# Held weights of eleven groups of stages at offsets of 8 to 112 bytes in place of one offset of 64 bytes, in a two-model transformer kernel on one core

## The chip, the cores and the metric

The kernel runs on one core of a Trainium2 chip. The time is the device time of one execution in microseconds (us); three runs give a median. One further execution was profiled, and every row below comes from it.

## The reference, cut to what matters

Fourteen sublayers run one after another on a sequence of 256 tokens of width 1024, in float32: a mixer, a cross-attention and a gated feed-forward net, twice, and then twice a feed-forward net, a three-branch mixer, a cross-attention and a second feed-forward net. Each ends in a residual sum and a layer norm. Nearly all of the arithmetic is products of the activations with weight matrices, such as

```
def swiglu_ffn(x, w_in, w_out):
    a, b = jnp.split(x @ w_in, 2, axis=-1)
    return (jax.nn.silu(a) * b) @ w_out
```

with a hidden width of 2816. Attention, scans and norms are small beside them.

## The kernel before, in words

A product is made of three matmuls in the type fp32r. Each operand is split into a high part (the value cast to fp32r) and a low part (the value less the high part), and the sum is high times high, low times high and high times low. All weights are 725 blocks of 128 partitions by 1024 words. `Stream._load` brings one into one of four staging tiles `w` by a DMA on SP's queue (lines 200 to 206). `Stream._split` casts it on ScalarE (L230) and subtracts on VectorE (L231) into one of ten slots of the pool `wp`, tile `w2`; the high part starts at `off`, the low part 1024 words, that is 4096 bytes, behind it. A slot is 2048 + 2*16 words, 8320 bytes, which is 65 times 128 bytes, so that all slots lie alike towards 128 bytes.

There are two ways to use a block. In `unit_group` (L360, L362, L364) the weights are held: a block of eight 128x128 pieces is loaded into the array piece by piece (a weight load, LDWEIGHTS) and the 256 columns of the activations `xT` stream past each (a MATMUL). One block makes 24 matmuls of 256 columns, called a unit here. `mm3` (L319 to L321) is also used with held weights, by the keys of a cross-attention (`x*_k`, `y*_k`), by the gates `e_g` and by the branches of the mixer (`m*_br`, which also come to 24 matmuls of 256 columns a block). In the other way, `mm3` holds activations (`xT`, `ph`, `pl`, or the memory's block) and streams the weights past: the down projections `_d`, the output projections `_o`, the values `_v` and the first 256 columns of a feed-forward net, `_t`.

The set `STANDING` names the endings of the held blocks; `stands(name)` tells whether a block is one. A block that is streamed, and the memory's block, lies at offset 0 of its slot; a held block lies at `HALF`, 16 words, that is 64 bytes. The pieces of a held block are 512 bytes apart and the pieces of `xT` 1024 bytes apart, so that towards 128 bytes each piece lies like the first.

The name of a block is the stage, an underscore and the part: `h10_g` is the gate and up projection of the feed-forward net `h10`. The stages run in the order e, x0, f0, o, x1, f1, h00, m0, y0, h01, h10, m1, y1, h11. Held blocks by stage: e has 17; x0 and x1 have 16 each (8 of `_q`, 8 of `_k`); f0, f1, h00, h01, h10 and h11 have 40 each (`_g`); o has 16 (`_qk`); m0 and m1 have 66 each (`qa` 4, `ckv` 1, `iq` 4, `ik` 1, `s` 8, `c` 12, `gate` 24, `br` 12); y0 and y1 have 8 each. That is 453 blocks. In a feed-forward net the order is gate unit, up unit, then 15 streamed matmuls of a down block of two units before, with the activation function in between on ScalarE and VectorE.

The order of the instructions on each engine is written out by the program; the blocks' order (`plan`) is recorded in a first pass and the loads and splits run ahead of their use by as many slots as are free (`pump`).

Of the kernel before, what the change touches and what calls it, by code (L numbers as in the profile page):

```python
# [168 lines left out]


HALF = 16


def stands(name):

    return name.split("_", 1)[-1] in STANDING
# [24 lines left out]
class Stream:  # L201
# [20 lines left out]
    def _split(self):  # L222
        n = self.net
        cols = self.plan[self.split][2]
        w = self.stage.pop(self.split)
        off = HALF if stands(self.plan[self.split][0]) else 0
        both = n.wp.tile([128, 2048 + 2 * HALF], F32R, tag="w2", name="w2")
        hi, lo = both[:, off:off + 1024], both[:, off + 1024:off + 2048]
        self._low()
        n.nc.scalar.copy(hi[:, :cols], w[:, :cols])  # L230
        self.due = lambda: n.nc.vector.tensor_sub(lo[:, :cols], w[:, :cols], hi[:, :cols].bitcast(F32))  # L231
        self.parts[self.split] = (hi, lo)
        self.split += 1
        self.live += 1
# [1364 lines left out]
```

## Time and profile before

| | us |
|---|---|
| median of 3 runs | 2263.19 |
| lowest and highest | 2262.1, 2263.37 |
| the profiled execution's own time | 2261.28 |
| its span, from first to last instruction | 2259.6 |
| TensorE busy in it | 2227.5 |
| VectorE busy | 1495.2 |
| ScalarE busy | 1155.4 |

The profiled execution lies 1.9 us under the median, and 1.7 us of its time lie outside the span. PE is TensorE's matmuls, PEld its weight loads, which overlap them; DVE is VectorE, ACT is ScalarE, POOL is GpSimd, SP the engine whose queue carries the loads. The matmuls are pipelined: one of 256 columns is shown with some 280 ns although the next one starts some 115 ns after it. So the pace is read from the starts of matmuls that follow one another, and not from their durations.

### The profile page before, as it was taken

What the parts mean: (1) busy time and instruction counts of PE and PEld (TensorE: products, weight loads), DVE (VectorE), ACT (ScalarE), POOL (GpSimd) and SP (SyncE); (2) the same over time, 40 slices, a digit from 0 to 9 for tenths busy, and PEclk for the clock granted to TensorE, in tenths of its full rate; (3) what the DMA queues carried; (4) which work ended last, traced back from release to release, by engine and by line L of the source; (5) the groups of instructions that cost most, each with busy time, mean ns of one, the idle gap of its engine ahead of it and who ended that gap; (6) DMA issues with size and microseconds to landing.
All of it is one profiled execution on the core that took longest, in us unless ns stands there. A gap on an engine that the chain in (4) does not pass through costs nothing.

```text
span 2259.6 us, 40982 instructions
## 1 busy us (share of the span) xinstructions
PE 2227.5 (99%) x16600; PEld 2083.7 (92%) x16600; DVE 1495.2 (66%) x2270; ACT 1155.4 (51%) x1856; POOL 203.7 (9%) x239
## 2 busy tenths in 40 slices
PE   8999999999999999999999999999999999999998
PEld 6989999988999999999899999999999899999998
DVE  5886665677657567656486677656656477677655
ACT  5555454378545444444745554444543845545542
POOL 0720000011000000000202100000000101200000
PEclk9999999999999999999999999999999999999999
DMA  8655476464446654764355655764764446555762
GB/s 235 169 168 168 151 255 191 154 207 138 159 151 233 191 186 166 229 190 152 131 179 158 198 176 192 231 189 136 253 192 144 159 144 183 169 194 167 258 191 77
DMA packets 118080, 407.50 MB, mean 180 GB/s; under 512 B 14169, under 2 KB 19418, under 8 KB 117890
## 3 DMA queue, kind: packets, MB, share of 16 engines
q1 hardware_dynamic: 116258, 402.00, 54.8%
q0 software_dynamic: 768, 1.57, 0.7%
q8 instruction: 130, 2.13, 0.4%
q10 hardware_dynamic: 864, 1.31, 0.2%
q14 instruction: 60, 0.49, 0.1%
HBM read 403.76 MB, written 1.06 MB: 179 GB/s over the span
## 4 chain that ended last, share of the span: by engine, by line
PE 91%; DVE 3%; ACT 3%; DMA 2%; issue 1%; POOL 1%; ACTq 0%; DVEq 0%; SPq 0%; POOLq 0%
PE ps L360 15%; PE ps L362 15%; PE ps L364 15%; PE acc L319 7%; PE acc L320 7%; PE acc L321 7%; PE ps L319 5%; PE ps L321 5%; PE ps L320 5%; DVE w L231 1%; PE ps L563 1%; PE ps L739 1%; PE ps L759 1%; ACT w L230 1%; DMA w<-in_o_qk 1%
## 5 line engine op out<-in xcount | busy, mean ns | idle before, releaser
L231 DVE TENSOR_TENSOR w<-w,w 128x1024 fp32r<-128x1024 f32 x725 | 883.3, 1238 | 363.5 <-ACT w L230 361.0
L360 PE MATMUL ps<-xT,w 128*128 128x256 f32 x3232 | 904.7, 280 | 0.0
L364 PE MATMUL ps<-xT,w 128*128 128x256 f32 x3232 | 897.1, 278 | 0.0
L362 PE MATMUL ps<-xT,w 128*128 128x256 f32 x3232 | 897.1, 278 | 0.0
L230 ACT CAST w<-w 128x1024 fp32r<-128x1024 f32 x725 | 748.4, 1051 | 223.7 <-PE ps L364 123.9
L360 PEld LDWEIGHTS ps<-xT,w 128*128 128x128 f32 x3232 | 608.2, 188 | 10.0 <-issue 5.5
L364 PEld LDWEIGHTS ps<-xT,w 128*128 128x128 f32 x3232 | 607.2, 188 | 0.0
L362 PEld LDWEIGHTS ps<-xT,w 128*128 128x128 f32 x3232 | 606.6, 188 | 0.6
L319 PE MATMUL acc<-w,ph 128*128 128x512 f32 (+1 forms) x940 | 329.5, 351 | 0.6 <-ACT ph L307 0.6
L320 PE MATMUL acc<-w,ph 128*128 128x512 f32 (+1 forms) x940 | 327.9, 349 | 0.0
L321 PE MATMUL acc<-w,pl 128*128 128x512 f32 (+1 forms) x940 | 327.6, 348 | 0.0
L319 PEld LDWEIGHTS acc<-w,ph 128*128 128x128 f32 x940 | 177.2, 189 | 25.7 <-ACT ph L307 0.8
L320 PEld LDWEIGHTS acc<-w,ph 128*128 128x128 f32 x940 | 177.0, 188 | 24.4
L321 PEld LDWEIGHTS acc<-w,pl 128*128 128x128 f32 x940 | 176.8, 188 | 24.2 <-DVE pl L308 0.2
L534 POOL TENSOR_TENSOR col<-col,mhalf 128x1 f32<-128x1 f32 (+1 forms) x38 | 28.5, 751 | 1559.2 <-DVE col L542 1437.1
L575 ACT ACTIVATE k<-ps 128x256 f32<-128x256 f32 x120 | 45.9, 383 | 160.4 <-PE ps L364 160.4
L304 ACT CAST ph<-k 128x256 fp32r<-128x256 f32 x120 | 48.8, 407 | 132.5 <-DVE k L577 132.5
L319 PE MATMUL ps<-w,w 128*128 128x256 f32 x384 | 111.8, 291 | 0.0
L319 PE MATMUL ps<-w,xT 128*128 128x256 f32 (+1 forms) x304 | 102.0, 336 | 9.2 <-ACT w L230 9.2
L321 PE MATMUL ps<-w,w 128*128 128x256 f32 x384 | 107.8, 281 | 0.0
L320 PE MATMUL ps<-w,w 128*128 128x256 f32 x384 | 107.5, 280 | 0.0
L576 DVE SCALAR_TENSOR_TENSOR k<-k,ps 128x256 f32<-128x256 f32 x120 | 50.4, 420 | 78.2 <-ACT k L575 78.2
(265 smaller groups left out, 2487.1 us busy)
## 6 DMA issues: line engine op xcount, KB each, us to landing
w<-in_h_g SPq DMA_DIRECT2D x160, 512.0 KB, 4.3
w<-in_h_d SPq DMA_DIRECT2D x88, 512.0 KB, 4.3
w<-in_f_g SPq DMA_DIRECT2D x80, 512.0 KB, 4.3
w<-in_m_gate SPq DMA_DIRECT2D x48, 512.0 KB, 3.9
w<-in_f_d SPq DMA_DIRECT2D x44, 512.0 KB, 4.2
gb<-in_ln_row SPq DMA_DIRECT2D x28, 512.0 KB, 6.8
w<-in_m_c SPq DMA_DIRECT2D x24, 512.0 KB, 3.2
w<-in_m_br SPq DMA_DIRECT2D x24, 512.0 KB, 3.6
```

The lines of the kernel that those rows point to most:

```text
L230: n.nc.scalar.copy(hi[:, :cols], w[:, :cols])
L231: self.due = lambda: n.nc.vector.tensor_sub(lo[:, :cols], w[:, :cols], hi[:, :cols].bitcast(F32))
L304: nc.scalar.copy(hi, src)
L319: mm(ps, a[0], b[0], start=first, stop=False)
L320: mm(ps, a[0], b[1], start=False, stop=False)
L321: mm(ps, a[1], b[0], start=False, stop=last)
L360: mm(ps, ws[i][0][:, k, :], xh[:, k, :], start=k == 0, stop=False)
L362: mm(ps, ws[i][1][:, k, :], xh[:, k, :], start=False, stop=False)
L364: mm(ps, ws[i][0][:, k, :], xl[:, k, :], start=False, stop=k == 7)
L534: self.nc.gpsimd.tensor_tensor(y, v, self.mhalf[:, :n], op=OP.pow)
L575: nc.scalar.activation(h, pg, AF.Tanh, scale=0.5)
L576: nc.vector.scalar_tensor_tensor(h, in0=h, scalar=1.0, in1=pg, op0=OP.add, op1=OP.mult)
```

## The change

The offset of a held block is taken from a table by the stage's name, in words of 4 bytes, with `HALF` for the stages that are not in it (e, y0, y1). For h01 and m1 the table has the 16 words of before. In bytes: f0 16, f1 32, h00 48, h01 64, h10 80, h11 96, m0 112, m1 64, x0 32, x1 96, o 8. Streamed blocks stay at 0. Nothing else changes, neither the instructions nor their order.

```
+BESIDE = dict(f0=4, f1=8, h00=12, h01=16, h10=20, h11=24, m0=28, m1=16, x0=8, x1=24, o=2)
...
-        off = HALF if stands(self.plan[self.split][0]) else 0
+        name = self.plan[self.split][0]
+        off = BESIDE.get(name.split("_")[0], HALF) if stands(name) else 0
         both = n.wp.tile([128, 2048 + 2 * HALF], F32R, tag="w2", name="w2")
         hi, lo = both[:, off:off + 1024], both[:, off + 1024:off + 2048]
```

## Rows read from the trace of the kernel before

**Rows 1.** The page: busy time of each engine, and the granted clock by slices.
```profile
PE 2227.5 (99%) x16600; PEld 2083.7 (92%) x16600; DVE 1495.2 (66%) x2270; ACT 1155.4 (51%) x1856; POOL 203.7 (9%) x239
...
PEclk9999999999999999999999999999999999999999
```

**Rows 2.** The page: the chain that ended last, shares by engine.
```profile
PE 91%; DVE 3%; ACT 3%; DMA 2%; issue 1%; POOL 1%; ACTq 0%; DVEq 0%; SPq 0%; POOLq 0%
```

**Rows 3.** Groups by line and form: busy us, mean ns, idle us before and releasers.
```profile
L360 PE MATMUL ps<-xT,w 128*128 128x256 f32 x3232 | 904.7, 280 | 0.0
...
L360 PEld LDWEIGHTS ps<-xT,w 128*128 128x128 f32 x3232 | 608.2, 188 | 10.0 <-issue 5.5 <-ACT sp L1180 0.7 <-ACT ph L304 0.7
```

**Rows 4.** Timeline of PE: start us, us, instruction. Two units: from first to next first.
```profile
741.67 0.28 PE L360 MATMUL ps<-xT,w 128*128 128x256 f32 x1
741.78 0.28 PE L362 MATMUL ps<-xT,w 128*128 128x256 f32 x1
741.90 0.28 PE L364 MATMUL ps<-xT,w 128*128 128x256 f32 x1
...
744.39 0.28 PE L360 MATMUL ps<-xT,w 128*128 128x256 f32 x1
...
758.16 0.28 PE L360 MATMUL ps<-xT,w 128*128 128x256 f32 x1
...
760.98 0.28 PE L360 MATMUL ps<-xT,w 128*128 128x256 f32 x1
```

**Rows 5.** Timeline of PE: the first and the last of the 404 units.
```profile
54.95 0.28 PE L360 MATMUL ps<-xT,w 128*128 128x256 f32 x1
...
57.77 0.28 PE L360 MATMUL ps<-xT,w 128*128 128x256 f32 x1
...
2232.64 0.28 PE L360 MATMUL ps<-xT,w 128*128 128x256 f32 x1
...
2235.36 0.40 PE L319 MATMUL acc<-w,ph 128*128 128x512 f32 x1
```

**Rows 6.** Timeline of PE: values of x1, memory's block held, weights streamed, both at 0.
```profile
620.48 0.28 PE L319 MATMUL ps<-w,w 128*128 128x256 f32 x1
...
623.33 0.49 PE L658 MATMUL ps<-sq,s 128*128 128x128 f32 x3
```

**Rows 7.** The chain in order of time, 208 to 220 us: start, us, what.
```profile
209.18 0.44 PE ps L658 x4
209.62 1.73 PE ps L739 x8
```

**Rows 8.** Windows: f0, f1, h00, h01, h10 whole; us, busy by engine (instructions), clock, DMA.
```profile
264.16:449.37 185.21, 185.21 (x1404) 176.60 (x1403) 120.13 (x156) 87.10 (x116) 4.05 (x4) 1.00 0.61 195
678.54:863.76 185.22, 185.22 (x1404) 176.54 (x1403) 120.03 (x156) 87.06 (x116) 4.07 (x4) 1.00 0.60 194
864.24:1049.41 185.17, 185.17 (x1404) 176.44 (x1403) 120.00 (x156) 86.99 (x116) 4.12 (x4) 1.00 0.61 197
1372.89:1558.71 185.82, 185.82 (x1404) 177.30 (x1402) 118.96 (x153) 86.90 (x116) 3.59 (x4) 1.00 0.60 193
1559.19:1744.87 185.68, 185.68 (x1404) 176.94 (x1403) 120.04 (x156) 86.69 (x116) 4.11 (x4) 1.00 0.61 196
```

**Rows 9.** Lines L230 and L231: duration ns min/median/max, first and last start.
```profile
L230 ACT CAST w<-w x725: 1027/1050/1092, 6.0 to 2226.3; 128x1024 fp32r<-128x1024 f32 x182
...
L231 DVE TENSOR_TENSOR w<-w,w x725: 1153/1225/2043, 7.1 to 2227.4; 128x1024 fp32r<-128x1024 f32 x182
```

**Rows 10.** Waits of PE: for whom, us in total, times, longest.
```profile
PE ps L319 <- ACT w L230: 9.2, 2, 7.1
PE ps L563 <- POOL x L550: 6.9, 10, 2.0
```

## The prediction

> **What bounds the kernel now.** I read the page's busy times first: PE is busy for 2227.5 of 2259.6 us, all of it at the high one of the two clocks, 2.4 GHz, in each of the 40 slices [rows 1]. The chain that ended last is PE for 91% of the span [rows 2], and the waits of PE for other engines are a few us in all [rows 10]. So the time is the number of matmuls by their pace, and whatever changes the pace of a long series of matmuls comes out in the total nearly whole.
>
> The mean durations do not tell the pace: 280 ns for a matmul of 256 columns [rows 3], while the next starts 110 to 120 ns on. The timeline does. In a unit of f1 24 matmuls take 744.39 - 741.67 = 2.72 us, 113.3 ns each; in another unit of the same stage they take 760.98 - 758.16 = 2.82 us, 117.5 ns each [rows 4]. Nothing waits in either, and both hold weights at the same 64 bytes. Inside a unit the step is steady from first to last, so there are two levels at which the stream can settle. The first of the 404 units is of the slow kind, 2.82 us, and the last of the fast kind, 2.72 us [rows 5]; over all 404, waits left out, the mean step is 115.1 ns, with about 61 in 100 steps at 113 or 114 ns and 38 in 100 at 117 ns or more.
>
> What differs where distance is zero? In the values of x1 the held block and the streamed one both lie at the start of a slot. There 24 matmuls of the same size take 623.33 - 620.48 = 2.85 us, 118.8 ns each [rows 6], more than either level of the held weights. A weight load (128 words a partition) runs while the matmul before it reads its 256 columns, and the two readers go through the same memory side by side. I take it that the difference between 118.8 and 115.1 ns, 3.7 ns a matmul, is what the 64 bytes now save, though the rows also differ in which tensor is held.
>
> **The change, part by part.** No instruction is added, removed or moved: same loads, splits and matmuls, same queues and waits. What changes is the start of held blocks in their slots. Held blocks with a new distance: 5 feed-forward nets of 40, m0 with 66, x0, x1 and o with 16 each, 314 in all, by 24 = 7536 matmuls. The other 139 (e 17, h01 40, m1 66, y0 and y1 8 each) keep 64 bytes and are the control.
>
> The trace has only two distances between a held fp32r block and what streams past it, 0 and 64 bytes. None of the new ones is shown, so the price of each is bounded from both sides. The upper end is the step at 0, 118.8 ns: 7536 x 3.7 = 28 us slower. The lower end is the fastest pace at which any 128-column load and matmul go here: four transposes take 0.44 us, 110 ns each, and eight attention matmuls of plain float32 and 256 columns take 1.73 us, 216 ns each or 108 ns a half [rows 7]; at 108 ns the 7536 would be 54 us faster. That end is far from every fp32r row. The nearer one is that all settle at the 113.3 ns of the fast unit: 1.8 x 7536 = 13.6 us faster.
>
> Between ends I take the row that each distance is nearest to, by a straight line: 64 bytes is the farthest that two places can be apart on a ring of 128, so a block 16 bytes from either end of the ring keeps a quarter of the saving, one at 32 a half, one at 48 three quarters. A unit has 24 x 3.7 = 89 ns to lose. Then f0 (16 bytes, three quarters of 40 x 0.089) loses 2.7 us; f1 (32) 1.8; h00 (48) 0.9; h10 (80) 0.9; h11 (96) 1.8; m0 (112, three quarters of 66) 4.4; x0 and x1 (32, 96) 0.7 each; o (8 bytes, seven eighths of 16) 1.2. The sum is 15.1 us. By the chain's share, 91% of it ends on the path: 13.7 us. In the feed-forward nets nothing can hide it, for PE is busy without a gap [rows 8]; in m0, o and the attention a part falls beside the waits of PE for a softmax or a load, which is what the other 9% stand for.
>
> The Trainium skill speaks against any effect at all: SBUF — State Buffer, section "Who interferes with whom", gives TensorE two independent read ports, one for the moving operand and one for the weight load, and says that it never waits on anyone. By that rule the sum would be nil; the two levels at one distance and the higher one at zero [rows 4, 6] do not look like it, but no row here changes the distance alone.
>
> The other edits cost nothing. The cast takes 1027 to 1092 ns for all 725 blocks, those at 0 and those at 64 bytes alike, and the subtraction has one median, 1225 ns, with a tail to 2043 [rows 9]; if a start at 8 bytes lengthened both by half, as no row says, it would be 0.5 and 0.6 us a block for o's 16 blocks, under a unit's 2.7 us. In a feed-forward net DVE is busy for 120 of 185 us and ACT for 87 [rows 8], so the splits have room; without it a unit would wait for its block, 1.2 us each. Loads, slots and the order on SP's queue are as before, and DMA writes the staging tiles, which don't move.
>
> **The sum.** The profiled execution took 2261.3 us, 1.9 under the median of 2263.2. 2261.3 + 13.7 = 2275.0, and against the median 2276.9. I say 2277.
>
> **The rivals.** First, no change (2259 to 2268): what counts is only that the two do not start alike, and every distance from 8 to 112 bytes does what 64 does. For it: the slow and the fast level both occur at 64, so which one a unit falls into hangs on more than the distance; the same stage at the same distance takes 185.17 us in h00 and 185.82 in h01 [rows 8], a drift of 0.65 us that needs no cause in the offsets. It is also what comes out where the two readers don't meet at all, so that rows 6 is slow for another reason, and where the slots' own place or the streamed tiles' place makes the distance another than the label says. Against it: the 3.7 ns would then jump within 8 bytes.
>
> Second, on the other side, faster: 64 bytes was one of the places, not the best, and other distances hold the stream at the fast level throughout. The place is the 24 matmuls of a unit; the price is 115.1 - 113.3 = 1.8 ns for each of 7536, 13.6 us, 12.4 on the path, and so 2250.8 against the median. It decides from a mean of 0.6 ns less on the 7536, 4.5 us, that is when a good third of the slow units turns fast with none turning slower. For it: 38 in 100 steps are slow now, so there is something to gain at some place, and the farthest place on the ring need not be the one where the load keeps clear of a stream that reads 256 words while it reads 128. Against it: all the new distances would have to be as good as the best of the old, while seven of the nine groups go nearer to zero by 32 bytes or more.
>
> The Trainium skill has a floor for this: TensorE: Matmul & The Clock Gate, section "Back-to-back issue gap", gives N/2.4 + 2.5 ns for an isolated matmul, 109.2 ns for 256 columns; an estimate by it is 5.9 x 7536 = 44 us of room. No fp32r row here comes to it.
>
> **How the numbers follow.** A measurement of this kernel tells about 0.2% from no change, 4.5 us. Slower, 0.52: the straight line, or a steeper one to 28 us. No change, 0.20. Faster, 0.28, most of it between 2250 and 2258, a little below where the floor is neared. The slow case's own range is 2268 to 2293. The range of the text reaches into the faster case to 2254 and ends above at 2293, the price of all 7536 at zero distance and a little more; about two in ten are left out, nearly all below.
>
> **What would show it.** In the new trace, units of f0, m0 and o at steps of 117.5 ns and more, those of h00 and h10 near the old mix, and the window of f0 longer by some 2.7 us than 185.2, of f1 by 1.8, while h01, m1, e and the streamed matmuls stay within 0.7 us a stage. Wrong: every feed-forward net within 0.7 us of before (the first rival), or f0, f1, h00, h10 shorter than 185 us (the second); a new wait for L230 or L231 in o would say that the splits and not the matmuls changed. The straight line is wrong if h00 at 48 and h10 at 80 bytes, equally far from zero, differ by more than 0.7 us.

## The result, and the profile after

The changed kernel took 2285.95 us (median of 4 runs, 2285.81 to 2286.53) against 2263.28 us of the kernel before beside it: a ratio of 1.0102, 95% interval 1.0087 to 1.0117, 22.7 us slower. Its profiled execution took 2286.03 us with a span of 2284.3, 24.7 us more than the span before. All line numbers of the kernel are two higher now: L362, L364 and L366 are the matmuls of a unit, L321 to L323 those of `mm3`, L232 and L233 the split.

The page of the changed kernel: busy times, granted clock, and the chain that ended last by engine.
```profile
PE 2253.2 (99%) x16600; PEld 2110.5 (92%) x16600; DVE 1499.1 (66%) x2270; ACT 1157.2 (51%) x1856; POOL 202.3 (9%) x239
...
PEclk9999999999999999999999999999999999999999
...
PE 93%; DVE 3%; ACT 2%; DMA 1%; issue 1%; POOL 1%; ACTq 0%; SPq 0%; DVEq 0%; POOLq 0%
```
Against [rows 1, 2] the instructions are the same in number, and every one of the 40 slices shows the same 9 for the clock. PE is busy 25.7 us longer, DVE 3.9 and ACT 1.8: the loss is in how fast matmuls follow one another.

The changed kernel's waits of PE (for whom, us, times, longest), and the lines of the split (ns min/median/max).
```profile
PE ps L321 <- ACT w L232: 8.9, 2, 7.1
PE ps L565 <- POOL x L552: 7.1, 11, 2.0
...
L232 ACT CAST w<-w x725: 1028/1050/1098, 6.0 to 2250.7; 128x1024 fp32r<-128x1024 f32 x182
...
L233 DVE TENSOR_TENSOR w<-w,w x725: 1154/1226/2037, 7.1 to 2251.7; 128x1024 fp32r<-128x1024 f32 x182
```
The waits and the split are those of [rows 9, 10]. Starts at 8, 16 or 112 bytes cost the writers nothing.

Windows of the changed kernel over whole stages (us, then busy by engine, clock, DMA share, GB/s): f0, f1, h00, h01, h10; then m0 and h11.
```profile
265.77:454.51 188.74, 188.74 (x1405) 180.03 (x1403) 120.47 (x156) 87.07 (x116) 4.05 (x4) 1.00 0.59 191
683.65:872.65 189.00, 189.00 (x1405) 180.38 (x1403) 120.37 (x156) 87.12 (x116) 4.07 (x4) 1.00 0.58 190
873.12:1061.24 188.12, 188.12 (x1405) 179.53 (x1403) 120.36 (x156) 87.09 (x116) 4.13 (x4) 1.00 0.59 194
1390.71:1576.55 185.84, 185.84 (x1404) 177.31 (x1403) 119.09 (x153) 86.74 (x116) 3.60 (x4) 1.00 0.60 193
1577.03:1764.79 187.76, 187.76 (x1404) 179.14 (x1403) 120.53 (x156) 87.26 (x116) 4.12 (x4) 1.00 0.59 194
...
1061.72:1331.87 270.15, 268.80 (x2037) 249.78 (x2035) 181.13 (x319) 149.99 (x260) 38.77 (x53) 1.00 0.51 164
2088.66:2276.68 188.02, 188.02 (x1400) 179.61 (x1398) 113.66 (x147) 82.61 (x111) 3.25 (x3) 0.99 0.52 168
```
The same two last windows of the kernel before.
```profile
1049.89:1313.90 264.01, 262.44 (x2037) 243.32 (x2035) 179.53 (x319) 149.87 (x260) 39.26 (x53) 1.00 0.52 168
2068.70:2251.96 183.26, 183.26 (x1401) 174.77 (x1399) 113.50 (x148) 82.29 (x111) 3.36 (x4) 1.00 0.53 173
```
Against [rows 8], f0 lost 3.5 us, f1 3.8, h00 2.95, h10 2.1, h11 4.8 and m0 6.1. h01, which kept its 64 bytes, took 185.84 us against 185.82. So the loss lies where the distance was changed, and in every large group where it was.

In h11 a part of it is something else. Its row shows a clock of 0.99, and this is how the stage starts in the changed kernel, and in the kernel before:
```profile
2088.66:2091.60 2.94, 2.94 (x16) 2.94 (x15) 1.83 (x3) 0.59 (x1) 0.00 (x0) 0.50 0.00 0
...
2068.70:2071.60 2.90, 2.90 (x27) 2.90 (x26) 1.97 (x4) 0.59 (x1) 0.10 (x1) 1.00 0.00 0
```
For some 3 us the granted clock was 0.50, the lower level of 1.2 GHz, and streamed matmuls that no edit touched stepped by 213 ns in place of 119. In both kernels PE had waited 2.0 us for the layer norm just before; why the clock was lower after it in one of them is open. That stretch costs 1.4 us of h11's 4.8, and the held matmuls 3.5. Such stretches come in some of the profiled executions below too, so the mean steps, which leave them out, tell more than the times do.

### The profile page after: what moved, and what is told of

The parts are those of the page before. It is cut to its first block, busy times and chain, and to the rows that moved or that the text cites. A ratio compares the mean times of both kernels' runs of the same rounds, so it can differ in the third digit from the quotient of the medians.

```text
span 2284.3 us, 40982 instructions
## 1 busy us (share of the span) xinstructions
PE 2253.2 (99%) x16600; PEld 2110.5 (92%) x16600; DVE 1499.1 (66%) x2270; ACT 1157.2 (51%) x1856; POOL 202.3 (9%) x239
## 4 chain that ended last, share of the span: by engine, by line
PE 93%; DVE 3%; ACT 2%; DMA 1%; issue 1%; POOL 1%; ACTq 0%; SPq 0%; DVEq 0%; POOLq 0%
PE ps L362 16%; PE ps L364 16%; PE ps L366 16%; PE acc L321 7%; PE acc L322 7%; PE acc L323 7%; PE ps L321 5%; PE ps L323 5%; PE ps L322 5%; PE ps L565 1%; PE ps L741 1%; PE ps L761 1%; DVE w L233 1%; DMA xq<-in_xT 1%; ACT w L232 1%
## 5 line engine op out<-in xcount | busy, mean ns | idle before, releaser
L233 DVE TENSOR_TENSOR w<-w,w 128x1024 fp32r<-128x1024 f32 x725 | 885.0, 1239 | 370.1 <-ACT w L232 367.1
L362 PE MATMUL ps<-xT,w 128*128 128x256 f32 x3232 | 911.8, 282 | 0.0
L364 PE MATMUL ps<-xT,w 128*128 128x256 f32 x3232 | 904.5, 280 | 0.0
L366 PE MATMUL ps<-xT,w 128*128 128x256 f32 x3232 | 904.3, 280 | 0.0
L232 ACT CAST w<-w 128x1024 fp32r<-128x1024 f32 x725 | 749.0, 1051 | 228.7 <-PE ps L366 128.6
L362 PEld LDWEIGHTS ps<-xT,w 128*128 128x128 f32 x3232 | 608.2, 188 | 10.0 <-issue 5.5
L364 PEld LDWEIGHTS ps<-xT,w 128*128 128x128 f32 x3232 | 608.1, 188 | 0.6 <-DVE w L233 0.2
L366 PEld LDWEIGHTS ps<-xT,w 128*128 128x128 f32 x3232 | 608.3, 188 | 0.0
L321 PE MATMUL acc<-w,ph 128*128 128x512 f32 (+1 forms) x940 | 329.7, 351 | 0.6 <-ACT ph L309 0.6
L323 PE MATMUL acc<-w,pl 128*128 128x512 f32 (+1 forms) x940 | 327.4, 348 | 0.0
L321 PEld LDWEIGHTS acc<-w,ph 128*128 128x128 f32 x940 | 177.2, 188 | 25.6 <-ACT ph L309 0.8
L323 PEld LDWEIGHTS acc<-w,pl 128*128 128x128 f32 x940 | 176.9, 188 | 24.3 <-DVE pl L310 0.2
L321 PE MATMUL ps<-w,w 128*128 128x256 f32 x384 | 112.1, 292 | 0.0
L321 PE MATMUL ps<-w,xT 128*128 128x256 f32 (+1 forms) x304 | 102.8, 338 | 8.9 <-ACT w L232 8.9
L323 PE MATMUL ps<-w,w 128*128 128x256 f32 x384 | 108.2, 282 | 0.0
```

The costliest lines, as they stand in the source:

```text
L321: mm(ps, a[0], b[0], start=first, stop=False)
L323: mm(ps, a[1], b[0], start=False, stop=last)
L362: mm(ps, ws[i][0][:, k, :], xh[:, k, :], start=k == 0, stop=False)
L364: mm(ps, ws[i][1][:, k, :], xh[:, k, :], start=False, stop=False)
L366: mm(ps, ws[i][0][:, k, :], xl[:, k, :], start=False, stop=k == 7)
```

## The experiments

The experiments test these theories of why a distance costs. A: the two readers of one memory, the weight load and the stream, get in each other's way according to their distance. B: as A, and evenly, the nearer the worse (the line of the prediction). C: unlike offsets in neighbouring slots cost, not the distance. D: the stage and what runs before it set the pace. E: only the weight load's own place counts. The pace in what follows is the mean step, from the start of one held matmul of 256 columns to the next start, with steps over 140 ns (waits, and matmuls at the lower clock) left out. A time with a ratio is a median of 4 to 11 runs; the others are of one execution.

**All held blocks at 0.**
```
-        off = BESIDE.get(name.split("_")[0], HALF) if stands(name) else 0
+        off = 0
```


> All held blocks go back to offset 0, as the streamed ones. Theory A (what counts is the place of the held piece towards the streamed one on a ring of 128 bytes, and 64 is the one good place): all 453 held blocks step at some 118.8 ns a matmul, as the values of x1 do in the kernel before, so 10,800 matmuls x 3.7 ns = 40 us above the kernel before, some 2303 us, and 17 us above the changed kernel. Rival B (64 is only the farthest, and the loss grows as the distance shrinks): the same 40 us, but then 48 and 80 bytes cannot cost what they cost in the changed kernel. Rival C (the mix of distances is what costs, since slots of unlike offsets follow one another): all at 0 is alike again and so no slower than the kernel before.

It took 2304.3 us, ratio 1.0185 (1.0170 to 1.0200), 41 us slower. The units of every stage came to 119.1 to 119.8 ns, those of the six feed-forward nets to 119.2 to 119.6. So 64 bytes is worth 41 us on 453 blocks, and C falls, since all slots are alike here and it is the slowest kernel of all. The timeline of PE in this kernel shows what the pace at 0 looks like: a unit of f0, the first matmul of its first piece, of its fourth, and of the next unit.
```profile
321.36 0.28 PE L362 MATMUL ps<-xT,w 128*128 128x256 f32 x1
...
322.44 0.28 PE L362 MATMUL ps<-xT,w 128*128 128x256 f32 x1
...
324.24 0.28 PE L362 MATMUL ps<-xT,w 128*128 128x256 f32 x1
```
2.88 us for 24, 120.0 ns each, and as even over its first three pieces (1.08 us for nine matmuls). The changed kernel's f0, at 16 bytes, does not settle on one step: its unit at 321.27 steps by 115 to 123 ns in a cycle of several matmuls and takes 2.85 us, 118.8 ns each.
```profile
321.27 0.28 PE L362 MATMUL ps<-xT,w 128*128 128x256 f32 x1
321.39 0.28 PE L364 MATMUL ps<-xT,w 128*128 128x256 f32 x1
321.51 0.28 PE L366 MATMUL ps<-xT,w 128*128 128x256 f32 x1
...
324.12 0.28 PE L362 MATMUL ps<-xT,w 128*128 128x256 f32 x1
```

**The distances given to other stages.**
```
-BESIDE = dict(f0=4, f1=8, h00=12, h01=16, h10=20, h11=24, m0=28, m1=16, x0=8, x1=24, o=2)
+BESIDE = dict(f0=24, f1=28, h00=4, h01=8, h10=12, h11=16, m0=20, m1=24, x0=16, x1=16, o=16)
```


> The distances are given to other stages: f0 96, f1 112, h00 16, h01 32, h10 48, h11 64, m0 80, m1 96 bytes, all else 64. Theory A (the distance sets the pace, whichever stage has it): mean steps of f0 117.4, f1 119.2, h00 118.7, h01 119.1, h10 118.1, h11 115, m0 117.8, m1 117.4 ns, each as in the stage that had the distance in the changed kernel; some 2288 us in all. Rival D (the stage and what runs before it set the pace): f0, f1, h00, h10 keep the 118.7, 119.1, 118.1, 117.8 ns that they have in the changed kernel, h01 and m1 stay at 115.9 and 114.9.

2281.6 us. Windows of this kernel: f0 at 96 bytes, f1 at 112, h00 at 16, h01 at 32, h10 at 48, h11 at 64.
```profile
264.09:451.25 187.16, 187.16 (x1405) 178.55 (x1403) 120.31 (x156) 87.05 (x116) 4.04 (x4) 1.00 0.60 193
679.34:868.46 189.12, 189.12 (x1405) 180.49 (x1403) 120.26 (x156) 86.85 (x116) 4.06 (x4) 1.00 0.58 190
868.94:1057.49 188.55, 188.55 (x1404) 179.90 (x1403) 120.48 (x156) 86.87 (x116) 4.12 (x4) 1.00 0.61 194
1384.76:1573.49 188.73, 188.73 (x1404) 180.13 (x1403) 119.53 (x153) 87.17 (x116) 3.59 (x4) 1.00 0.59 190
1573.97:1762.14 188.17, 188.17 (x1404) 179.53 (x1403) 120.38 (x156) 86.84 (x116) 4.12 (x4) 1.00 0.59 194
2089.06:2272.31 183.25, 183.25 (x1400) 174.76 (x1398) 113.81 (x148) 82.55 (x111) 3.35 (x4) 1.00 0.53 173
```
Mean steps: 117.2, 119.2, 118.6, 119.0 and 118.2 ns at 96, 112, 16, 32 and 48 bytes, against 117.4, 119.2, 118.7, 119.1 and 118.1 in the stages that had them in the changed kernel; m0 at 80 came to 117.7 (h10 had 117.8) and m1 at 96 to 117.3. The pace goes with the distance, within 0.3 ns, and D falls for these distances. h11, back at 64, took 183.25 us against 183.26 before. The total was 6 us under the forecast, 1.2 us of it since that h11 steps at 113.7 and not at the 115 that I had put in. What runs before does count at 64 bytes: the 96 units' matmuls each of y0 and y1, at 64 in both kernels, stepped by 116.8 and 117.8 ns before and by 115.6 and 115.8 in the changed kernel.

**Near 64 and near 0.**
```
+BESIDE = dict(f0=15, f1=17, h00=14, h01=18, h10=2, h11=1, m0=16, m1=30, x0=16, x1=16, o=16)
```


> Near 64 and near 0: f0 60, f1 68, h00 56, h01 72, h10 8, h11 4, m1 120 bytes, all else 64. Theory A1 (a dip at 64 itself): 60 and 68 already step at 117 ns or more. Theory A2 (a dip some 16 bytes wide, a piece's place within 16 bytes does not count): 60 or 68, whichever is in the same 16 bytes as 64, stays at 115 and 72 with it, 56 does not. Rival B (a straight line from 0 to 64): 60 and 68 at 115.3, 56 and 72 at 115.6, 8 at 118.3, 4 at 118.6 ns. For 8 bytes the changed kernel had 117.0 ns in o, so h10 at 117 under A and 118.3 under B; m1 at 120 bytes as 8 if the ring is even on both sides.

2287.1 us. 60 bytes came to 118.9 ns, 68 to 118.1, 56 to 117.8, 72 to 118.2, 8 to 116.9, 4 to 118.6 and 120 to 118.4. A step of one word off 64 loses 3.0 to 3.8 of the 4.2 ns that lie between 64 and 0. That ends B, and A2 with it.

**The rest of the ring**, in two kernels.
```
+BESIDE = dict(f0=6, f1=10, h00=22, h01=26, h10=3, h11=13, m0=31, m1=19, x0=16, x1=16, o=16)
```


> The rest of the ring: f0 24, f1 40, h00 88, h01 104, h10 12, h11 52, m0 124, m1 76 bytes, all else 64. Theory A1 (64 alone is good, by its steady step of 272 clocks): all eight at 117 to 119.5 ns; those at odd multiples of 8 bytes (24, 40, 88, 104) perhaps a little lower, as 8 and 56 were (116.9, 117.8); in all some 2287 us. Rival B (a straight line): 52 and 76 at 115.8, 40 and 88 at 116.5, 24 and 104 at 117.4, 12 and 124 at 118 to 119 ns.

2284.6 us, and two of the eight refuted A1: 52 bytes (h11) came to 115.1 ns and 76 (m1) to 114.7. Both have the steady cycle of 64. This is a unit of h11 at 52 bytes in the timeline of PE: first matmul, that of the third piece, that of the last, and the next stream.
```profile
2147.86 0.28 PE L362 MATMUL ps<-xT,w 128*128 128x256 f32 x1
...
2148.55 0.28 PE L362 MATMUL ps<-xT,w 128*128 128x256 f32 x1
...
2150.25 0.28 PE L362 MATMUL ps<-xT,w 128*128 128x256 f32 x1
2150.59 0.40 PE L321 MATMUL acc<-w,ph 128*128 128x512 f32 x1
```
From 2148.55 on a piece of three takes 0.34 us, 113.3 ns a matmul, as in the fast unit of [rows 4]. The others came to 118.7 (24), 118.5 (40), 116.9 (88), 118.9 (104), 117.3 (12) and 119.5 (124).
```
+BESIDE = dict(f0=25, f1=21, h00=23, h01=9, h10=7, h11=19, m0=13, m1=27, x0=19, x1=13, o=19)
```


> More of the ring: f0 100, f1 84, h00 92, h01 36, h10 28, h11 76, m0 52, m1 108 bytes; x0 and o 76, x1 52. So far 52 (115.1), 64 (115.1) and 76 (114.7 ns) have the steady level of 272 clocks for most steps, and 88 and 12 for a third. Theory C (good places 12 bytes apart around 64, wearing off): 76 and 52 good here too, in h11, m0, x0, o and x1, at 115 to 116 ns; 100 and 36 or 28 like 88, some 117; 84, 92, 108 at 118 to 119. Theory D (in the earlier map the two stages came out low by what ran before them): 76 in h11 and 52 in m0 at 117.5 ns or more.

2290.8 us. 52 was good again in m0 (114.7 ns) and x1 (115.4), and 76 in o (114.8) and, less, in h11 (115.9); x0 at 76 had 116.9. 100, 84, 92, 36, 28 and 108 came to 119.7, 118.6, 119.4, 118.8, 118.4 and 119.9. So C of that forecast holds for 52 and 76 and for nothing beyond. In sum, over 29 distances: 52, 64 and 76 at 113.7 to 116.9 ns (y0 and y1 aside); 8, 12, 88 and 96 at 116.9 to 117.4; the rest at 117.7 to 119.9, with no trend between. Counted by units, twelve steps on end at 113 or 114 ns occur at 52, 64 and 76 in most of them, at 88 in 14 of 40, at 40 in 7 of 40, and nowhere else. Of the units that the change moved, none has them.

A distance here is one towards 128 bytes. The slots are 8320 bytes apart, 32 and a half times 256, so that towards 256 bytes every other slot lies 128 bytes further, and each figure is a mean over both halves. It can matter: if the blocks take the ten slots in turn, 12 of the 14 steady units at 88 bytes lie in one half of the slots (115.5 ns against 118.4 in the other). The halves were not tested by themselves.

**xT moved in place of the weights**, and once more with each part of it moved alike.
```
-        off = BESIDE.get(name.split("_")[0], HALF) if stands(name) else 0
+        off = 0
...
-            self.xT = [self.one.tile([128, 8, S], F32R, tag=f"xT{i}", name="xT") for i in range(2)]
+            self.xT = [self.one.tile([128, 8 * S + 32], F32R, tag=f"xT{i}", name="xT")[:, 16:16 + 8 * S]
+                       .rearrange("p (k c) -> p k c", k=8) for i in range(2)]
```


> The activations xT start 64 bytes further and all held weights go back to 0, so that for the 404 units the distance is 64 again but with the weights at the place that cost 40 us when all of it was at 0. Theory A (the distance between the two readers counts): units at 115 ns; the branches and the keys, whose streamed side stays at 0, at 119; the 576 streamed matmuls of the first 256 columns of the feed-forward nets, whose held side is xT, at 116.5 instead of 118.9; in all 2263 + 576 x 4.2 ns + 576 x 2.7 ns - 576 x 2.2 ns = 2266 us, 2264 to 2268. Rival E (the weight load's own place counts, 64 is good and 0 is bad): as with all held blocks at 0, 2303 us.

2288.1 us, ratio 1.0104 (1.0091 to 1.0118): between the two forecasts. The feed-forward nets stepped at 117.8 ns, better than the 119.3 of 0 and worse than 115.1. I had overlooked that the low part of `xT` lies behind the high part, so that it moved by the padding as well, by 192 bytes and not by 64. The second kernel moves both by 64, with held weights at 0 as in the first:
```
-                       ... for i in range(2)]
+            self.xT = [self.one.tile([128, 8 * S + n], F32R, tag=f"xT{i}", name="xT")[:, o:o + 8 * S]
+                       .rearrange("p (k c) -> p k c", k=8) for i, (n, o) in enumerate(((16, 16), (48, 0)))]
```


> As the kernel with xT moved and held weights at 0, but here both parts of xT move by exactly 64 bytes and every other tile keeps its place towards 256 bytes; in the earlier one the high part moved by 64 and the low part by 192, because the tile in front of it had grown. Theory A256 (the distance counts on a ring of 256, with 64 ahead and 64 behind apart, so that the earlier kernel mixed both signs): the units come back to 115 to 116 ns with the steady level of 113.3, some 2267 us. Rival H (the place of each reader counts for itself beside the distance, or the sign of the distance): units at 117.8 ns again, 2288 us.  Under both the tiles behind, and the streamed matmuls that hold xT, stay as in the earlier kernel.

2268.4 us. Windows of f0 and f1 in the first of these two kernels:
```profile
267.52:454.98 187.46, 187.46 (x1404) 178.99 (x1403) 120.14 (x156) 87.02 (x116) 4.05 (x4) 1.00 0.60 193
684.57:871.92 187.35, 187.35 (x1405) 178.74 (x1403) 119.99 (x156) 86.52 (x116) 4.05 (x4) 1.00 0.60 191
```
and of the same two in the second:
```profile
266.06:450.94 184.88, 184.88 (x1404) 176.30 (x1403) 120.12 (x156) 87.12 (x116) 4.06 (x4) 1.00 0.61 195
680.30:865.34 185.04, 185.04 (x1405) 176.44 (x1402) 119.83 (x156) 87.13 (x116) 4.07 (x4) 1.00 0.60 194
```
184.88 and 185.04 us, the 185.2 of [rows 8] again, with held weights at 0. E falls: the place of the weights that cost 41 us costs nothing once what streams past them has moved too. And 128 bytes is not the whole of it: with the low part of `xT` 128 bytes further off than the high part, the steady cycle is not reached in any of the 404 units.

**The low part of the weights alone at 0.**
```
-        off = BESIDE.get(name.split("_")[0], HALF) if stands(name) else 0
-        hi, lo = both[:, off:off + 1024], both[:, off + 1024:off + 2048]
+        off, down = (HALF, HALF) if stands(name) else (0, 0)
+        hi, lo = both[:, off:off + 1024], both[:, off + down + 1024:off + down + 2048]
```


> Only the low part of a held block moves, from 64 to 0 towards 128 bytes; high parts stay at 64. One of the three matmuls per piece is then a load from 0. Theory F (each matmul pays for its own distance): a mean step of 2/3 x 115.1 + 1/3 x 119.2 = 116.5 ns, 2263 + 10,800 x 1.4 ns = 2278 us. Theory G (what 64 buys is a steady state of the whole stream, in which every step is like the last, and one odd load in three breaks it): the fast level of 113.3 ns is gone altogether and the mean step is 117.5 ns or more, 2289 us or above.

2291.5 us, f0 188.02 us against 185.21, mean steps of 118 ns in f0. G it is: one load in three from another place spoils the other two, and no unit has twelve steps on end at 113 or 114 ns. What 64 bytes buys is a cycle in which every step is like the last.

**Streamed blocks at 64 too.**
```
+        off = 0 if name.startswith("mem") else HALF
```


> All weight blocks lie at 64 bytes, the streamed ones too; only the memory's block stays at 0. What a streamed block streams past (xT, ph, pl, the memory) lies at 0, so its distance becomes 64. Theory A (the distance between held and streamed counts, whichever of the two is moved): the streamed matmuls of 256 columns go from 118.8 to some 115 ns, 2279 x 3.7 = 8 us, and those of 512 columns from 231 by 4 to 7 ns, 2028 x that = 8 to 14 us; in all some 2244 to 2250 us, faster than the kernel before. Rival E (only the held piece's own place counts, as a start at 64 bytes for the weight load): nothing changes, 2263 us, within 2 us.

2266.0 us, ratio 1.0014 (1.0004 to 1.0024): a little slower, where A promised 13 to 19 us. The total is nearer to E's forecast, but not by E's reason, for streamed matmuls of 256 columns went from 118.8 to 116.3 ns, which is half of A's mechanism. Those of 512 did not gain (231.1 to 231.4 ns). And held units paid back what was won, at the same distance as ever: the 404 units went from 115.1 to 115.8 ns, 6.5 us. Windows of f1 and h11 in this kernel:
```profile
676.62:862.68 186.06, 186.06 (x1404) 177.26 (x1403) 120.08 (x156) 87.03 (x116) 4.06 (x4) 1.00 0.60 193
2068.22:2255.55 187.33, 187.33 (x1401) 178.64 (x1399) 113.70 (x148) 82.53 (x111) 3.29 (x4) 0.99 0.53 169
```
h11 took 4.1 us more than before, 1.3 of it in a stretch at the lower clock as above and 2.9 by the mean step of its units, 116.7 against 113.7 ns. Counting units by their first steps shows why: of the 96 that come right behind a streamed matmul of 256 columns of a down or output projection, 47 started at the fast level before and 26 here. A unit right behind a fast unit stayed fast in every case, 110 of 110 and 84 of 84; behind a slow one 22 of 73 and 12 of 99 turned fast. So the fast level is handed on, and the streamed matmuls before a unit have a part in which level it starts at.

**Only values and output projections at 64**, chosen since no unit stands right behind most of them.
```
+        off = HALF if stands(name) or name.split("_", 1)[-1] in ("v", "o") else 0
```


> Beside the held blocks only the values and the output projections lie at 64 bytes; the down projections and the first columns, which run right before units, stay at 0. If the gain of the streamed matmuls of 256 columns (2.5 ns each) is had without pushing the units that follow into the slow level: 576 x 2.7 for the values and 336 x 2.0 for the outputs, 2.2 us below the kernel before, 2261 us. If the units after them lose the fast level as those after the down projections did: no gain, 2263 us or a little more.

2260.7 us, ratio 0.9989 (0.9980 to 0.9998): the fastest of all, 2.7 us under the kernel before by the medians, at the edge of what can be told. The values of the attentions went from 119.0 to 116.3 ns; the units of f0, f1, h00, h01, h10 and h11 kept their steps to 0.01 ns. The profiled execution itself took 2264.6 us, with h01 and h11 starting at the lower clock, 1.5 us each; so from it steps are read and not times.

**Held at 76, with that.**
```
+        part = name.split("_", 1)[-1]
+        off = 19 if stands(name) else HALF if part in ("v", "o") else 0
```


> All held blocks at 76 bytes, values and output projections at 64, the rest at 0. If 76 lets a unit reach the steady level more often than 64 (75 in 100 steps against 64 in m1): the 404 units at 114.7 ns in place of 115.1, 4 us, and the 2 us of the values and outputs kept, 2257 us. If the level is set by what runs before the units and not by 76 against 64: 2261 us. The keys, which meet the memory's block at 0, may come out either way, 576 matmuls x 2 ns = 1 us.

2267.1 us, ratio 1.0020 (1.0011 to 1.0029). The fast level is reached more often (in f0 64 steps in 100 at 113 or 114 ns, 60 before), but the steps that miss it are at 121 and 126 ns here and not at 118: f0 116.4, h11 115.9 ns. 64 stays the best of the places tried for all held blocks.

**The change with m0 alone put back.**
```
-... m0=28, ...
+... m0=16, ...
```


> The change with m0 alone put back from 112 to 64 bytes; the other eight groups keep their new distances. If the groups add up, each paying its own matmuls times its own step: m0's held matmuls took 194.1 us in the changed kernel and 187.9 before, so 6.2 us come back, 2285.9 - 6.2 = 2279.7 us, and no other stage moves by more than 0.5 us. If a stage's level hangs on the stages before it: y0, h01 and later stages move by a us or more beside it, in either direction.

2281.5 us, ratio to the kernel before 1.0078 (1.0061 to 1.0094). Windows of m0 and h01:
```profile
1063.39:1327.58 264.19, 262.20 (x2037) 243.09 (x2035) 180.26 (x319) 149.82 (x260) 38.33 (x53) 1.00 0.53 168
1386.45:1572.28 185.83, 185.83 (x1405) 177.30 (x1403) 119.20 (x153) 87.01 (x116) 3.60 (x4) 1.00 0.59 193
```
m0 gave back 6.0 us and the steps of no other held group moved it by more than 0.2: the groups add up. By the medians 4.5 us came back. The profiled execution lost 1.5 us near its start, where the granted clock from 20 to 27 us was 0.56 against 0.76 in the changed kernel and PE took up 17 matmuls in place of 24; whether the other runs did so is not shown.

## Why the prediction was right, and where it was not

**The bound** was right: PE by its pace. The waits that I called a few us in all come to 24 us, most of them at the start and behind the layer norms. I let 9% of the loss vanish beside waits, and about that much did: by their mean steps the moved matmuls cost some 25.5 us, and 23.3 came out, most of the difference in o and m0. The other 1.4 us of the span's 24.7 are the stretch at the lower clock in h11, which the prediction had not.

**The direction** was right, and so was the upper price. I took the step at 0 from streamed values, 118.8 ns; held at 0 it is 119.3 ns. That the result lies within the range is owed to this end, the price of all 7536 at zero distance, and not to the line that gave the 2277.

**The size** failed at one step, "I take the row that each distance is nearest to, by a straight line". It priced the 7536 moved matmuls at 2.0 ns each in the mean, and they cost 3.4. Stage by stage, forecast and measured (windows; held matmuls for h11, x0, x1, o):

| group, bytes | forecast us | measured us |
|---|---|---|
| f0, 16 | 2.7 | 3.5 |
| f1, 32 | 1.8 | 3.8 |
| h00, 48 | 0.9 | 2.95 |
| h10, 80 | 0.9 | 2.1 |
| h11, 96 | 1.8 | 3.5 |
| m0, 112 | 4.4 | 6.1 |
| x0, 32 | 0.7 | 1.1 |
| x1, 96 | 0.7 | 0.8 |
| o, 8 | 1.2 | -0.5 |
| sum | 15.1 | 23.3 |

Nearness has no part in it. 48 and 80 bytes lose most of the saving, 8 is among the better places, and 60 is as bad as 16. The units of h00 and h10, which I had near the old mix of levels, have lost the fast level altogether. o's matmuls stepped 1.5 ns slower and its waits shrank by more. My own test of the line, that h00 and h10 must not differ by more than 0.7 us, failed too: 2.95 and 2.1.

**The first rival**, that any distance but zero does what 64 does, is refuted by every large group. What I gave for it, the 0.65 us between h00 and h01 as a drift without a cause, was a misreading: h11 took 183.26 and 183.25 us in two different kernels, and unit steps repeat to 0.01 ns. The mix of levels is not drawn anew in each execution; with the same program before it, it comes out the same.

**The second rival**, that other places hold the fast level, had a true core: 52 and 76 do. But none of the change's own distances is one of them.

**Whether distance can count.** By the Trainium skill's SBUF — State Buffer, "Who interferes with whom", the two read ports are independent and TensorE waits for no one. Here the same instructions at the same clock step by 113.3 to 120.0 ns with only addresses changed, so the measurement decides: these fp32r pairs do not run as if the two were independent. The step of an isolated matmul by the Trainium skill's TensorE: Matmul & The Clock Gate, "Back-to-back issue gap", an estimate of 109.2 ns, was not reached by any steady cycle of these runs. I had called it a floor, which that section does not.

**What stays open.** Which part of the memory the two readers share, if it is one, and why most units settle at 52, 64 and 76, a third of them at 88 and none at 12. The runs show the pattern, that it goes beyond 128 bytes, and the handing on of the level; why the places are these was not tried.

## What to carry to other kernels

Where a kernel streams at TensorE's pace, read the steps between matmul starts by stage: at one clock and with no wait they differed by 5% here, by addresses alone. Place held and streamed operands at one measured distance for all parts, high and low alike; don't interpolate between two distances, since one word off the good place lost 3 ns or more of the 4. Before a stage's time is put down to a change, read its granted clock, for 3 us at the lower level made up almost a third of h11's loss here. Count what comes behind a change of place as well, for a stream that gains can leave the next one in a slower cycle.

## What the runs showed that I had not expected

- Good places are one word wide: 115.1 ns at 64 bytes, 118.9 at 60 and 118.1 at 68, with two more at 52 and 76.
- The steady cycle needs all three matmuls of a piece at the same distance: 118 ns with one in three moved, and 117.8 with the low part of `xT` 128 bytes further than the high part.
- A unit behind a fast unit was fast in 110 of 110 cases, and the pattern repeats between executions and kernels: 113.72 ns in h11 in three of them.
- Matmuls of 512 columns, at 231 ns, did not care: 230.8 to 231.4 ns at 0 and at 64.
- Runs of 3 us at the lower clock behind a wait of 2 us come and go between executions: one at the start of h11 in the changed kernel's profile and none in the profile before, two in that of the kernel with values and output projections at 64. Each costs 1.4 to 1.5 us there.
